# An encoder layer: six products of the values ahead of a branch, four of them read behind it; the sums of X on VectorE; two small PSUM banks for three uses

## The chip, the core and the metric

The kernel runs on one core of one Trainium2 chip. The metric is the device time of one execution in microseconds. A core has five engines with their own instruction queues: TensorE (PE in the profile, with PEld for its weight loads), VectorE (DVE), ScalarE (ACT), GpSimd (POOL) and SyncE (SP), which here issues the transfers. They meet through semaphores. TensorE writes into PSUM, which has eight banks of 128 x 512 float32; VectorE and ScalarE read them.

## The reference

One layer of a bidirectional encoder over x of 2048 x 1024 float32, then a final RMSNorm:

```python
h = _rmsnorm(x, norm_w[layer])
proj = jnp.einsum('bsd,de->bse', h, w_in[layer])           # 1024 -> 10 x 1024 columns
(q_raw, ffwd_raw, fbwd_raw, i_raw, ga_raw,
 u_raw, v_raw, gb_raw, ma_raw, mb_raw) = jnp.split(proj, split_points, axis=-1)
y_a = _hgrn2_branch(q_raw, ffwd_raw, fbwd_raw, i_raw, ga_raw, ...)   # gated linear recurrence, both ways
# branch B:
u = jax.nn.gelu(u_raw)
v = _layernorm(jax.nn.gelu(v_raw), ln_w, ln_b)
mixed = jnp.einsum('gts,bnsgc->bntgc', w_s, vc) + b_s.T[None, None, :, :, None]
y_b = u * mixed.reshape(b, s, SG_WIDTH) * jax.nn.silu(g_raw)
merged = (jax.nn.sigmoid(ma_raw) * jnp.einsum('bsw,wd->bsd', y_a, w_proj_a[layer])
          + jax.nn.sigmoid(mb_raw) * jnp.einsum('bsw,wd->bsd', y_b, w_proj_b[layer]))
x = x + jnp.einsum('bsd,de->bse', merged, w_out[layer])
return _rmsnorm(x, final_norm_w)
```

## The kernel before

The normed x lies transposed in SBUF as four tiles xT of 512 positions, each value as the sum of two float16 numbers (high and low part). A product of two such operands takes three matmuls for each 128 rows of the contraction (high x high, high x low, low x high).

The stages follow one another on TensorE:

1. `phase1` (lines 297 to 423): the columns of the recurrence, and the recurrence itself. At its end the first two products of the values are made (`self.first`).
2. `values` (827 to 894): the columns `v_raw`, 16 tiles of 128 positions in two halves of 512 columns. A half is one product of 24 matmuls into a bank of the pool `p_v` (five banks, tile `pin`), read by ScalarE with the gelu into a tile V (three buffers); VectorE takes the statistics (line 844); after the second half VectorE aggregates them, GpSimd makes the reciprocal deviation (850, 851), VectorE norms the tile (852) and SP stores it to DRAM (854).
3. `branch_b`: gates and mixing. `merge_gates`: the two merge gates. `branch_a`: the gate path of the recurrence. `final`: the projections, the merge, the output.

**The branch.** The recurrence is computed by a short way that holds while its numbers stay in a range. Behind the products of three tiles (`early = 3`, lines 856 to 862) `range_flag` loads a flag into a register on every engine, and `exact()` repeats the recurrence in a safe way where the flag is set. With these inputs it isn't set. Each engine has a branch instruction there, and then an instruction that sets its semaphore as if the block had run. In `exact` too, products go through the five banks of `pin`.

**Seven products.** From `branch_b` on, a product of 2 x 2 blocks is made with seven block products (Winograd's form), written out in `seven` (752): twelve matmuls each into one of three banks of a side, which `copy` and `take` read on ScalarE and VectorE. That needs sums of blocks of both operands. For X these are made beside the values: `x_parts(p, k)` (613) adds the high and low parts of X into a buffer `raw` (two adds on GpSimd, line 619), makes the sums there (`z_sums`, three operations on VectorE, line 642) and splits them into high and low parts (ScalarE 626, VectorE 627). `raw` and `tmp` have one buffer each. `x_last(p, k)` (629) makes the last sum in place in xT. For weights and for later operands the class `Make` (658) does the like: `load` (DMA), `square` and `scale` (a common power of two, from the sum of squares), `sums`, `split`. Its steps are hung into slots: `side_by_side` (797) runs product n of each generator and then the functions in slot n.

**Small PSUM tiles.** `scale` (718) adds up over the partitions with a matmul into the bank `misc` (one buffer), which VectorE reads (`pow2`, line 130). `px` (one buffer) takes the mixing products of branch B (957, read by 959), the bias (900) and the transposes of branch A (1162, read by 1164). With the six banks of the seven products that makes eight.

**The order.** Tile, the library the kernel is written in, plans each engine's order ahead of time: it runs the program through a cost model, gives each engine what is ready, first what comes first in the program, and writes a fixed order with all semaphore waits. An instruction may so be planned ahead of one that stands before it in the program. At run time every engine works through its list in that order.

Of the kernel before, what the change touches and what calls it, by code (L numbers as in the profile page):

```python
# [17 lines left out]
F32 = mybir.dt.float32  # L18
# [6 lines left out]
PSUM = bass.MemoryType.PSUM  # L25
# [26 lines left out]
class Trunk:  # L52
# [9 lines left out]
    def consts(self):  # L62
        nc, tc, ctx = self.nc, self.tc, self.ctx
        c = self.c = ctx.enter_context(tc.tile_pool(name="consts", bufs=1))
        self.sm = ctx.enter_context(tc.tile_pool(name="small", bufs=4))
        self.dram = ctx.enter_context(tc.tile_pool(name="scratch", bufs=1, space=DRAM))
        self.pg = ctx.enter_context(tc.tile_pool(name="p_misc", bufs=1, space=PSUM))
        self.plan()

        self.ident = c.tile([P, P], F32, name="ident")  # L70
        make_identity(nc, self.ident)
        self.ones = c.tile([P, P], F32, name="ones")
        nc.vector.memset(self.ones, 1.0)
        self.ones16 = c.tile([P, P], BF16, name="ones16")
        nc.vector.memset(self.ones16, 1.0)
        self.mhalf = c.tile([P, 1], F32, name="mhalf")
        nc.vector.memset(self.mhalf, -0.5)
# [535 lines left out]
    def x_parts(self, p, k):  # L613

        nc = self.nc
        raw, tmp = self.rt.tile([P, 2, 2, SEG], F32, name="raw"), self.rt.tile([P, 3, SEG], F32, name="tmp")
        for i in range(2):
            x = self.xT[2 * p + i]
            nc.gpsimd.tensor_tensor(out=raw[:, :, i], in0=x[:, 0, 2 * k:2 * k + 2], in1=x[:, 1, 2 * k:2 * k + 2],
                                    op=ALU.add)  # L620
        flat = raw.rearrange("p h i t -> p (h i) t")
        self.z_sums(flat, tmp, s3=False)
        xs = self.xs[p][k // 2]
        for dst, src in ((slice(0, 1), flat[:, 1:2]), (slice(1, 3), tmp[:, 1:3])):
            hi, lo = (xs[:, a, dst, k % 2] for a in range(2))
            nc.scalar.activation(out=hi, in_=src, func=AF.Copy)
            nc.vector.tensor_tensor(out=lo, in0=src, in1=hi, op=ALU.subtract)

    def x_last(self, p, k):

        nc = self.nc
        r = self.vw.tile([P, 2, SEG], F32, name="V")
        xs = [self.xT[2 * p + i][:, :, 2 * k] for i in range(2)]
        for i in range(2):
            nc.vector.tensor_tensor(out=r[:, i], in0=xs[i][:, 0], in1=xs[i][:, 1], op=ALU.add)
        nc.vector.tensor_tensor(out=r[:, 0], in0=r[:, 0], in1=r[:, 1], op=ALU.subtract)
        nc.scalar.activation(out=xs[1][:, 0], in_=r[:, 0], func=AF.Copy)
        nc.vector.tensor_tensor(out=xs[1][:, 1], in0=r[:, 0], in1=xs[1][:, 0], op=ALU.subtract)

    def z_sums(self, raw, tmp, s3=True, part=(0, 1)):  # L640

# [16 lines left out]
    class Make:  # L658
# [3 lines left out]
            self.s, self.inv = scale or (None, None)  # L662

        def load(self):
            self.raw = self.rt.tile([P, 2, 1024], F32, name="raw")
            self.tmp = self.rt.tile([P, 3, SEG], F32, name="tmp")
            self.flat = self.raw.rearrange("p h n -> p (h n)")
            self.src(self.raw)

        def square(self):  # L670
            sm, tr = self.tr.sm, self.tr
            ss = sm.tile([P, 2], F32, name="wss2")
            junk = self.tmp.rearrange("p i n -> p (i n)").bitcast(F16)
            for h in range(2):
                self.nc.scalar.activation(out=junk[:, 1024 * h:1024 * h + 1024], in_=self.raw[:, h],  # L675
                                          func=AF.Square, accum_out=ss[:, h:h + 1])
            self.sb = sm.tile([P, 2], BF16, name="wsb2")
            self.nc.gpsimd.tensor_copy(out=self.sb, in_=ss)
# [2 lines left out]
            self.s, self.inv = self.tr.scale([self.sb[:, i:i + 1] for i in range(2)], ("ws7", "winv7"), 12)  # L681

        def sums(self, i):
            if self.kind == "z":
                return self.tr.z_sums(self.raw.rearrange("p h (i t) -> p (h i) t", i=2), self.tmp, part=(i,))
            b11, b12, b21, b22 = self.blocks
            t2, t3, t4 = (self.tmp[:, j] if len(b11.shape) == 2 else
                          self.tmp[:, j].rearrange("p (k n) -> p k n", n=P) for j in range(3))
            sub = lambda out, x, y: self.nc.vector.tensor_tensor(out=out, in0=x, in1=y, op=ALU.subtract)  # L689
            if i == 0:  # L690
                sub(t3, b22, b12)
                sub(b12, b12, b11)
            else:
                sub(t2, b22, b12)
                sub(t4, b21, t2)
# [22 lines left out]
    def scale(self, sums, names, bufs):  # L718

        nc, sm = self.nc, self.sm  # L720
        pb = self.pg.tile([P, 1], F32, name="misc")
        for i, sb in enumerate(sums):
            nc.tensor.matmul(pb, self.ones16, sb, start=(i == 0), stop=(i == len(sums) - 1))  # L723
        s = sm.tile([P, 1], F32, name=names[0], bufs=min(bufs, 3))
        inv = sm.tile([P, 1], F32, name=names[1], bufs=bufs)
        self.pow2(s, inv, pb, room=1)
        return s, inv

    def make_w(self, w, c0, u, rt, scale=None):

# [96 lines left out]
    def values(self):  # L827
# [1 line left out]
        wv = [self.wv, self.unit(self.w_in, C_V + SEG, ahead=0)]  # L829
        V, st, order = {}, {}, self.v_order  # L830

        def half(t, u):
            b, n = order[t] // 4, order[t] % 4
# [3 lines left out]
            if u == 0 and t < len(self.first):  # L837
                ps = self.first[t]
            else:
                ps = self.pin.tile([P, SEG], F32, name="pin")  # L840
                self.proj_wide(ps, wv[u][0], self.xT[b], slice(n * P, n * P + P))
            v = V[t][:, 4 * u:4 * u + 4].rearrange("p g c -> p (g c)")
            nc.scalar.activation(out=v, in_=ps, func=AF.Gelu_apprx_tanh, scale=wv[u][1])  # L843
            nc.vector.bn_stats(out=st[t][:, u], in_=v)
            if u == 0:
# [5 lines left out]
            nc.gpsimd.tensor_tensor(out=r, in0=r, in1=self.mhalf, op=ALU.pow)  # L851
            nc.vector.tensor_scalar(out=V[t], in0=V[t], scalar1=mv[:, 0:1], scalar2=r,
                                    op0=ALU.subtract, op1=ALU.mult)
            nc.sync.dma_start(out=self.v_d[b][:, :, n, :], in_=V[t])

        early = 3
        for u in range(2):
            for t in range(early):
                half(t, u)
        flag = self.range_flag()  # L860
        with tc.If(flag > 0):
            self.exact()
        right = dict(side="right", reuse_waits="tile")
        xs = self.ctx.enter_context(tc.tile_pool(name="xs", bufs=4, **right))
        self.xsp = xs
# [3 lines left out]
        self.own = [self.make_w(*x) for x in self.x_units()]  # L869
        first, second = self.own[0:2]  # L870
        for t in range(early, NT):
            for u in range(2):
                half(t, u)

            if 3 <= t < 11:
                self.x_parts((t - 3) // 4, (t - 3) % 4)
            if 7 <= t < 15:
                self.x_last((t - 7) // 4, (t - 7) % 4)
            if t == 11:
                first.load()  # L880
            elif t == 12:
                first.square()
                first.scale()
            elif t == 13:
                first.sums(0)
                first.sums(1)
            elif t == 14:
                for i in range(4):
                    first.split(i, self.w7)
# [6 lines left out]
    def mixing_bias(self, i, wsT, bsb):  # L896

        nc = self.nc
        pr = self.pq.tile([P, 4, P], F32, name="px")
# [28 lines left out]
    def branch_b(self):  # L928

        nc, tc, sm = self.nc, self.tc, self.sm  # L930
        with ExitStack() as es:
# [16 lines left out]
            for u in range(4):  # L948
                y = {}
                order = [(p, i, j) for i, j in ((0, 0), (1, 1), (0, 1), (1, 0)) for p in range(2)]  # L950
                def mix(p, i, j):
                    b, g = 2 * p + i, 2 * u + j
                    v = vl.tile([P, 4, P], F32, name="vl")
                    nc.sync.dma_start(out=v, in_=self.v_d[b][:, g])
                    px = self.pq.tile([P, 4, P], F32, name="px")
                    for n in range(4):
                        nc.tensor.matmul(px[:, n, :], v[:, n, :], wsT[:, g, :], start=True, stop=True)
                    y[p, i, j] = yp.tile([P, 4, P], F32, name="y")
# [67 lines left out]

    def make_z(self, kind, p, k, rt):
        src = lambda raw: self.nc.sync.dma_start(out=raw, in_=self.y_d[kind][p][k].rearrange("p h i t -> p h (i t)"))
        return self.Make(self, src, rt, self.zscale[kind, p], "z")

    def merge_gates(self):

# [123 lines left out]
    def ga_group(self, side, p, u, unit):  # L1156
        nc = self.nc

        def turn(o, sg, i, j):
            pt = self.pq.tile([P, 4, P], F32, name="px")  # L1160
            for n in range(4):
                nc.tensor.transpose(pt[:, n, :], o[:, n, :], self.ident)
            y = o.rearrange("p n t -> p (n t)")
# [32 lines left out]
    def final(self, z, last):  # L1196
# [4 lines left out]
        for n in range(6):  # L1201
# [4 lines left out]
            else:  # L1206
                zk = ((1, 0), (1, 1), (2, 0), (2, 1), None)[n - 1]
                zn = [None] * 4
                if zk:
                    self.z_scale(*zk)  # L1210
                    mk = [self.make_z(*zk, k, self.rt) for k in range(4)]
                    mk[0].load()
            xo = None
            for u in range(4):
                slots = {}
# [3 lines left out]
                if mk:  # L1219
                    m = mk[u]  # L1220

                    def begin(m=m):
# [2 lines left out]
                        pool = next(self.z_from)  # L1225
                        m.split(0, pool)

                    slots = {1: [begin], 2: [lambda m=m: m.split(1)], 3: [lambda m=m: m.split(2)],
                             4: [lambda m=m: m.split(3)] + ([mk[u + 1].load] if u < 3 else [])}
                if kind < 2:  # L1230
                    if W[u] is None:
                        W[u] = self.pb[3].t, self.pb[3].inv
# [193 lines left out]
    def run(self):  # L1426
# [14 lines left out]
        self.mb_d = blocks("mb")  # L1441
        self.kept, self.zscale, self.rot = {}, {}, [(0, 1, 2), (0, 1, 2)]
        self.xTp = ctx.enter_context(tc.tile_pool(name="xTp", bufs=NSEG))
        with tc.tile_pool(name="p_in", bufs=2, space=PSUM) as self.pin, tc.tile_pool(name="wu", bufs=5) as self.wu:
            self.phase1()
            with tc.tile_pool(name="p_v", bufs=5, space=PSUM, reuse_waits="tile") as self.pin, \
                    tc.tile_pool(name="vw", bufs=3, reuse_waits="tile") as self.vw:
# [52 lines left out]
```

## Time and profile before

| | |
|---|---|
| time, median of 3 runs | 2433.22 us (2428.64 to 2433.70) |
| the profiled execution: its own time | 2434.28 us |
| its span, first to last instruction | 2432.5 us |
| TensorE busy | 2334.8 us |
| VectorE / ScalarE / GpSimd busy | 1535.1 / 1020.4 / 315.9 us |
| mean granted TensorE clock | 0.992 |
| moved by DMA | 281.26 MB |

Times in the profile count from the first instruction. A row of a timeline has the start, the duration, the engine, the line of the kernel, the operation, the tile it writes and those it reads, the shapes, the count, and in brackets the idle time of that engine ahead of it with what ended it. A row by line has the count, shortest, median and longest duration in ns, and first and last start. A row of a list of waits has who waited for whom, the total, the count and the longest. The suffix q on an engine means its sequencer. A row of a stretch has start and end, its length, and then for each engine the busy time and count.

### The profile page before, as it was taken

Reading aid. Unit: us, or ns where it says so; the run is one execution under the profiler, and the core shown is the slowest. Engines: PE = TensorE matmul, PEld = TensorE weight load, DVE = VectorE, ACT = ScalarE, POOL = GpSimd, SP = SyncE. Lnnn points to the kernel's source line nnn. Section 1 sums busy time; section 2 is a strip of 40 time slices with the busy share of each in tenths; the row PEclk is TensorE's granted clock in tenths of the full one; section 3 lists DMA queues with packets and bytes.
Section 4 is the critical chain, followed back from the end, with each engine's and each line's share of the span. In section 5 each row is a group of like instructions: output and inputs, shape, how many; then the busy total and the mean of one; then the engine's idle time right before and its main releaser. Section 6 shows DMA issues by size and latency. Waiting matters only on the chain. (4 is left out here: it accounts for less than half of the span.)

```text
span 2432.5 us, 33850 instructions
## 1 busy us (share of the span) xinstructions
PE 2334.8 (96%) x12880; PEld 1299.2 (53%) x12880; DVE 1535.1 (63%) x3014; ACT 1020.4 (42%) x1871; POOL 315.9 (13%) x523
## 2 busy tenths in 40 slices
PE   7999999999999999899999999899999999999998
PEld 5666766685668566444444554344444444444443
DVE  5687548745872677567456456577765554576754
ACT  6533332433332334323345446566564532244432
POOL 2222202220211121351000000000000000000011
PEclk9999999999999999999999999999999999999999
DMA  5200110011001001112322222677665674777733
GB/s 176 77 10 27 36 35 10 27 36 36 14 23 47 6 18 53 46 52 79 121 88 90 83 87 95 221 260 265 245 201 171 215 268 148 276 239 263 241 122 119
DMA packets 169486, 281.26 MB, mean 116 GB/s; under 512 B 10976, under 2 KB 105184, under 8 KB 162144
## 3 DMA queue, kind: packets, MB, share of 16 engines
q1 hardware_dynamic: 169312, 278.98, 33.7%
q8 instruction: 104, 1.70, 0.3%
q14 instruction: 70, 0.57, 0.1%
HBM read 174.08 MB, written 104.86 MB: 115 GB/s over the span
## 5 line engine op out<-in xcount | busy, mean ns | idle before, releaser
L794 PEld LDWEIGHTS <-seven 128*128 128x128 f16 x5376 | 525.4, 98 | 640.5 <-issue 32.0
L794 PE MATMUL bank<-seven 128*128 128x512 f16 x2016 | 441.2, 381 | 8.7 <-DVE zs L808 6.4
L794 PE MATMUL bank<-xT,seven 128*128 128x512 f16 x1920 | 429.3, 380 | 4.8 <-ACT zs L761 2.6
L794 PE MATMUL bank<-xs,seven 128*128 128x512 f16 x1440 | 321.1, 380 | 0.0
L217 PE MATMUL pin<-xT,wsplit 128*128 128x512 f16 x768 | 291.1, 379 | 0.2 <-DVE wsplit L204 0.2
L215 PE MATMUL pin<-xT,wsplit 128*128 128x512 f16 x768 | 291.0, 379 | 0.2 <-ACT xT L279 0.2
L216 PE MATMUL pin<-xT,wsplit 128*128 128x512 f16 x768 | 291.1, 379 | 0.0
L215 PE MATMUL pin<-wsplit,xT 128*128 128x256 f16 (+1 forms) x768 | 240.3, 313 | 9.5 <-ACT V L843 5.0
L216 PE MATMUL pin<-wsplit,xT 128*128 128x256 f16 (+1 forms) x768 | 240.7, 313 | 3.2 <-DVE wsplit L204 3.2
L217 PE MATMUL pin<-wsplit,xT 128*128 128x256 f16 (+1 forms) x768 | 240.5, 313 | 2.3 <-DVE xT L280 2.1
L808 DVE SCALAR_TENSOR_TENSOR zs<-bank,us,zs 128x512 f32<-128x512 f32 x120 | 88.9, 746 | 76.6 <-PE bank L794 74.0
L815 ACT ACTIVATE zs<-zs 128x512 f32<-128x512 f32 x120 | 75.3, 627 | 140.0 <-DVE zs L808 139.7
L808 DVE SCALAR_TENSOR_TENSOR zs<-bank,su,zs 128x512 f32<-128x512 f32 x72 | 53.9, 749 | 110.0 <-PE bank L794 86.4
L217 PEld LDWEIGHTS <-wsplit 128*128 128x128 f16 x768 | 75.1, 98 | 90.2 <-DVE wsplit L204 0.7
L502 POOL TENSOR_TENSOR q<-ff,e 128x512 f32<-128x512 f32 x64 | 73.6, 1150 | 371.7 <-DVE e L500 231.0
L216 PEld LDWEIGHTS <-wsplit 128*128 128x128 f16 x768 | 75.1, 98 | 77.5
L215 PEld LDWEIGHTS <-wsplit 128*128 128x128 f16 x768 | 75.4, 98 | 75.7
L689 DVE TENSOR_TENSOR tmp<-raw 128x512 f32<-128x512 f32 x64 | 43.9, 690 | 111.9 <-ACT tmp L675 104.5
L455 ACT ACTIVATE fz<-pin,wus 128x512 f32<-128x512 f32 x64 | 43.9, 686 | 143.1 <-PE pin L217 142.9
L761 ACT ACTIVATE zs<-bank,us 128x512 f32<-128x512 f32 x120 | 80.1, 676 | 56.0 <-PE bank L794 53.5
L216 PEld LDWEIGHTS <-xT 128*128 128x128 f16 x768 | 76.5, 100 | 44.7 <-issue 9.7
L217 PEld LDWEIGHTS <-xT 128*128 128x128 f16 x768 | 76.4, 99 | 44.2 <-DVE xT L280 5.0
(202 smaller groups left out, 3614.5 us busy)
## 6 DMA issues: line engine op xcount, KB each, us to landing
kept<-seven SPq DMA_DIRECT2D x16, 1792.0 KB, 7.9
seven<-kept SPq DMA_DIRECT2D x16, 1792.0 KB, 9.4
wraw<-in_w_in_dram SPq DMA_DIRECT2D x20, 1024.0 KB, 5.1
raw<-in_w_in_dram SPq DMA_DIRECT2D x40, 512.0 KB, 4.8
xt<-in_x_dram SPq DMA_DIRECT2D x16, 512.0 KB, 4.2
o_d<-ob SPq DMA_DIRECT2D x32, 256.0 KB, 2.3
v<-V SPq DMA_DIRECT2D x16, 512.0 KB, 3.5
vl<-v SPq DMA_DIRECT2D x32, 256.0 KB, 2.8
```

Of the source, the lines that this page charges most:

```text
L215: nc.tensor.matmul(ps, lh(k), rh(k), start=(k == 0), stop=False)
L216: nc.tensor.matmul(ps, lh(k), rl(k), start=False, stop=False)
L217: nc.tensor.matmul(ps, ll(k), rh(k), start=False, stop=(k == KT - 1))
L455: nc.scalar.activation(out=fz[:, 1:SEG + 1], in_=ps, func=AF.Sigmoid, scale=us)
L502: nc.gpsimd.tensor_tensor(out=q0.rearrange("p (m c) -> p m c", c=64), in0=ff.rearrange("p (m c) -> p m c", c=64), in1=e8.rearrange("p n b ...
L689: sub = lambda out, x, y: self.nc.vector.tensor_tensor(out=out, in0=x, in1=y, op=ALU.subtract)
L761: self.nc.scalar.activation(out=t, in_=ps, func=AF.Copy, scale=su)
L794: nc.tensor.matmul(ps, lhs(x, k), rhs(y, k), start=start and not (k or n), stop=k == 3 and n == 2, skip_group_check=True)
L808: self.nc.vector.scalar_tensor_tensor(out=more, in0=ps, scalar=su, in1=more, op0=ALU.mult, op1=ALU.add)
L815: self.nc.scalar.activation(out=out, in_=more, func=func)
```

## The change

Four things are changed.

- `values`: `half` is split into `product` (the matmuls) and `norm` (gelu, statistics, norming, store). Six products are still made ahead of the branch, but only the two that `phase1` made are read there; the other four are read behind `exact()`.
- `x_parts` and `x_last` become generators of two steps, one after each half of a tile; the two adds of `x_parts` go from GpSimd to VectorE. `x_last` runs one tile later (tiles 8 to 15), and so does the scale of the first weight unit.
- The bank `misc` lives until the end of the values. From then on `scale` takes its bank from the pool of `px`, which gets two buffers.
- `Make.load` takes only `raw`; `tmp` is taken when it is first needed. In `final`, a piece is begun at slot 2 in place of 1 (but for the fourth unit), the next is loaded one slot earlier, after the second split, and the first piece of the next group is loaded in slot 4 of the fourth unit, ahead of its scale.

```diff
     def x_parts(self, p, k):
...
-            nc.gpsimd.tensor_tensor(out=raw[:, :, i], in0=x[:, 0, 2 * k:2 * k + 2], in1=x[:, 1, 2 * k:2 * k + 2],
+            nc.vector.tensor_tensor(out=raw[:, :, i], in0=x[:, 0, 2 * k:2 * k + 2], in1=x[:, 1, 2 * k:2 * k + 2],
                                     op=ALU.add)
         self.z_sums(flat, tmp, s3=False)
+        yield
...
         def load(self):
-            self.raw = self.rt.tile([P, 2, 1024], F32, name="raw")
-            self.tmp = self.rt.tile([P, 3, SEG], F32, name="tmp")
+            self.raw, self.tmp = self.rt.tile([P, 2, 1024], F32, name="raw"), None
...
     def scale(self, sums, names, bufs):
-        pb = self.pg.tile([P, 1], F32, name="misc")
+        pb = self.px()[:, 0, 0:1] if self.pq else self.pg.tile([P, 1], F32, name="misc")
...
+    def px(self):
+        return self.pq.tile([P, 4, P], F32, name="px", bufs=2)
...
         early = 3
+        ps = {}
         for u in range(2):
             for t in range(early):
-                half(t, u)
+                ps[t, u] = product(t, u)
+                if u == 0 and t < len(self.first):
+                    norm(t, u, ps[t, u])
         flag = self.range_flag()
         with tc.If(flag > 0):
             self.exact()
+        for t in range(early):
+            for u in range(int(t < len(self.first)), 2):
+                norm(t, u, ps[t, u])
...
         for t in range(early, NT):
+            parts = ([self.x_parts((t - 3) // 4, (t - 3) % 4)] if 3 <= t < 11 else []) + \
+                    ([self.x_last((t - 8) // 4, (t - 8) % 4)] if 8 <= t else [])
             for u in range(2):
-                half(t, u)
-            if 3 <= t < 11:
-                self.x_parts((t - 3) // 4, (t - 3) % 4)
-            if 7 <= t < 15:
-                self.x_last((t - 7) // 4, (t - 7) % 4)
+                norm(t, u, product(t, u))
+                for x in parts:
+                    next(x)
             if t == 11:
                 first.load()
             elif t == 12:
                 first.square()
+            elif t == 13:
                 first.scale()
-            elif t == 13:
                 first.sums(0)
...
     def final(self, z, last):
-                    mk[0].load()
+                    early.s, early.inv = mk[0].s, mk[0].inv
+                    mk[0] = early
...
-                    slots = {1: [begin], 2: [lambda m=m: m.split(1)], 3: [lambda m=m: m.split(2)],
-                             4: [lambda m=m: m.split(3)] + ([mk[u + 1].load] if u < 3 else [])}
+                    at = 2 if u < 3 else 1
+                    slots = {at: [begin], at + 1: [lambda m=m: m.split(1)], at + 2: [lambda m=m: m.split(2)],
+                             at + 3: [lambda m=m: m.split(3)]}
+                    if u < 3:
+                        slots[at + 1].append(mk[u + 1].load)
+                if u == 3 and n < 4:
+                    early = self.make_z(*((1, 0), (1, 1), (2, 0), (2, 1))[n], 0, self.rt)
+                    slots.setdefault(4, []).append(early.load)
...
-        with tc.tile_pool(name="p_in", bufs=2, space=PSUM) as self.pin, tc.tile_pool(name="wu", bufs=5) as self.wu:
+        self.pq = None
+        with tc.tile_pool(name="p_misc", bufs=1, space=PSUM, reuse_waits="tile") as self.pg, \
+                tc.tile_pool(name="p_in", bufs=2, space=PSUM) as self.pin, tc.tile_pool(name="wu", bufs=5) as self.wu:
```

More of the change, by code (lines that the diff above doesn't have):

```diff
@@ L627, in x_parts @@
             nc.vector.tensor_tensor(out=lo, in0=src, in1=hi, op=ALU.subtract)
+        yield
     def x_last(self, p, k):
@@ L636, in x_last @@
         nc.vector.tensor_tensor(out=r[:, 0], in0=r[:, 0], in1=r[:, 1], op=ALU.subtract)
+        yield
         nc.scalar.activation(out=xs[1][:, 0], in_=r[:, 0], func=AF.Copy)
         nc.vector.tensor_tensor(out=xs[1][:, 1], in0=r[:, 0], in1=xs[1][:, 0], op=ALU.subtract)
+        yield
     def z_sums(self, raw, tmp, s3=True, part=(0, 1)):
@@ L664, in load, with need @@
         def load(self):
-            self.raw = self.rt.tile([P, 2, 1024], F32, name="raw")
-            self.tmp = self.rt.tile([P, 3, SEG], F32, name="tmp")
+            self.raw, self.tmp = self.rt.tile([P, 2, 1024], F32, name="raw"), None
             self.flat = self.raw.rearrange("p h n -> p (h n)")
             self.src(self.raw)
+        def need(self):
+            if self.tmp is None:
+                self.tmp = self.rt.tile([P, 3, SEG], F32, name="tmp")
         def square(self):
+            self.need()
             sm, tr = self.tr.sm, self.tr
@@ L683, in sums @@
         def sums(self, i):
+            self.need()
             if self.kind == "z":
@@ L830, in values, with product, norm @@
         V, st, order = {}, {}, self.v_order
-        def half(t, u):
-            b, n = order[t] // 4, order[t] % 4
+        def product(t, u):
+            if u == 0 and t < len(self.first):
+                return self.first[t]
+            ps = self.pin.tile([P, SEG], F32, name="pin")
+            self.proj_wide(ps, wv[u][0], self.xT[order[t] // 4], slice(order[t] % 4 * P, order[t] % 4 * P + P))
+            return ps
+        def norm(t, u, ps):
             if u == 0:
@@ L836, in half @@
                 st[t] = sm.tile([P, 2, 6], F32, name="bst")
[L837 to L841, printed above, removed]
             v = V[t][:, 4 * u:4 * u + 4].rearrange("p g c -> p (g c)")
@@ L853, in half @@
                                     op0=ALU.subtract, op1=ALU.mult)
-            nc.sync.dma_start(out=self.v_d[b][:, :, n, :], in_=V[t])
+            nc.sync.dma_start(out=self.v_d[order[t] // 4][:, :, order[t] % 4, :], in_=V[t])
         early = 3
+        ps = {}
         for u in range(2):
             for t in range(early):
-                half(t, u)
+                ps[t, u] = product(t, u)
+                if u == 0 and t < len(self.first):
+                    norm(t, u, ps[t, u])
         flag = self.range_flag()
@@ L898, in mixing_bias @@
         nc = self.nc
-        pr = self.pq.tile([P, 4, P], F32, name="px")
+        pr = self.px()
         nc.tensor.matmul(pr, self.ones, wsT[:, 4 * i:4 * i + 4, :], start=True, stop=True)
@@ L954, in mix @@
                     nc.sync.dma_start(out=v, in_=self.v_d[b][:, g])
-                    px = self.pq.tile([P, 4, P], F32, name="px")
+                    px = self.px()
                     for n in range(4):
@@ L1028, in make_z @@
         src = lambda raw: self.nc.sync.dma_start(out=raw, in_=self.y_d[kind][p][k].rearrange("p h i t -> p h (i t)"))
-        return self.Make(self, src, rt, self.zscale[kind, p], "z")
+        return self.Make(self, src, rt, self.zscale.get((kind, p)), "z")
     def merge_gates(self):
@@ L1159, in turn @@
         def turn(o, sg, i, j):
-            pt = self.pq.tile([P, 4, P], F32, name="px")
+            pt = self.px()
             for n in range(4):
```

1 line of the change is left out of this document (removed).

## The prediction

> **What bounds the kernel now.** I read the page first, then TensorE's list of waits, then the stretches around the edits.
>
> ```profile
> span 2432.5 us, 33850 instructions
> PE 2334.8 (96%) x12880; PEld 1299.2 (53%) x12880; DVE 1535.1 (63%) x3014; ACT 1020.4 (42%) x1871; POOL 315.9 (13%) x523
> ```
>
> TensorE (PE) is busy for all but 97.7 us (2432.5 - 2334.8), and no matmul is removed. So a gain can only come out of those 97.7 us, or out of matmuls that ran at a lowered clock just behind a pause. The list of TensorE's waits says which part of them the edits touch:
>
> ```profile
> PE bank L794 <- DVE zs L808: 8.5, 8, 2.1
> PE px L957 <- DVE y L959: 7.8, 4, 3.7
> PE pin L215 <- ACT V L843: 5.0, 3, 3.1
> PE bank L794 <- ACT zs L761: 4.9, 8, 0.9
> PE misc L723 <- DVE p2t L130: 4.5, 1, 4.5
> PE pin L215 <- ACTq L861: 4.5, 1, 4.5
> PE px L1162 <- DVE zs L1164: 4.0, 5, 1.6
> ```
>
> The columns are the wait in total, how often, and the longest. Rows 2 and 7 are the one px bank, row 5 the one misc bank, row 6 the branch, row 3 the sums of X. Rows 1 and 4 are spread over the stages of the seven products, most of them in the last one.
>
> **The branch.** The sequencers' rows of line 861, two of TensorE's timeline, one of ScalarE's:
>
> ```profile
> L861 PEldq COMPARE_BRANCH  x1: 4883/4883/4883, 1010.0 to 1010.0; - x1
> L861 POOLq COMPARE_BRANCH  x1: 45/45/45, 1011.7 to 1011.7; - x1
> L861 POOLq EVENT_SEMAPHORE  x1: 17/17/17, 1014.7 to 1014.7; - x1
> L861 ACTq COMPARE_BRANCH  x1: 50/50/50, 1014.8 to 1014.8; - x1
> L861 PEldq EVENT_SEMAPHORE  x1: 51/51/51, 1015.0 to 1015.0; - x1
> L861 ACTq EVENT_SEMAPHORE  x1: 17/17/17, 1017.9 to 1017.9; - x1
> 1013.50 0.69 ACT L843 ACTIVATE V<-pin,wus 128x512 f32<-128x512 f32 x1 [4.28 <-PE pin L217]
> 1017.95 0.38 PE L215 MATMUL pin<-wsplit,xT 128*128 128x512 f16 x1 [4.49 <-ACTq L861]
> 1021.79 0.38 PE L216 MATMUL pin<-wsplit,xT 128*128 128x512 f16 x1
> ```
>
> TensorE is through its own branch at 1015.0 but starts at 1017.95, when ScalarE has passed: ScalarE had to read the sixth product (1013.50) before it could branch (1014.8), and an engine needs about 3 us from branch to next instruction (GpSimd 1011.7 to 1014.7, ScalarE 1014.8 to 1017.9). The edit moves four reads (ScalarE), their four statistics and three tile norms (VectorE, GpSimd) and three stores of V (SP's queue) behind the branch. All engines but TensorE can then branch while the products run, so that TensorE waits for its own branch alone: 1015.0 in place of 1017.95, 2.9 us.
>
> The pause also costs clock. From 1017.95 to 1021.79 ten matmuls took 3.84 us. At full speed they are 0.2157 us apart, from the row of 24:
>
> ```profile
> 1161.45 5.34 PE L794 MATMUL bank<-xT,seven 128*128 128x512 f16 x24
> ```
>
> (5.34 - 0.38) / 23 = 0.2157, so ten are 2.16 us and 1.7 us were lost. A pause of 1.6 us (1013.46 to 1015.0) should not lower it: after the pause of 1.67 quoted below the matmul is at 0.38. Together 4.6 us; bounds 0 (if the reads stay in front) and 4.6.
>
> The Trainium skill (Advanced Engine Details and Errata, Control Flow Timing) gives about 108 ns for a compare-and-branch. By it ScalarE would have been through at 1014.9, and this term would be 0 and the time 4.6 us higher. The rows disagree: 3.1 us on ScalarE, 3.0 on GpSimd. The skill's page Runtime: NRT & Kernel Launch (Instruction fetch mechanics) has a taken branch out of the loaded pages wait for a fetch, which fits them.
>
> **The sums of X.** GpSimd's adds move to VectorE, in steps:
>
> ```profile
> L619 POOL TENSOR_TENSOR raw<-xT x16: 2116/2129/3111, 1018.0 to 1081.0; 128x1024 f32<-128x1024 f16 x16
> 1079.32 2.76 DVE L627 TENSOR_TENSOR xs<-tmp,xs 128x1024 f16<-128x1024 f32 x1 [0.52 <-ACT xs L626]
> 1087.90 1.23 DVE L627 TENSOR_TENSOR xs<-tmp,xs 128x1024 f16<-128x1024 f32 x1 [1.12 <-ACT xs L626]
> L642 DVE TENSOR_TENSOR tmp<-raw x56: 679/691/694, 1024.3 to 2318.4; 128x512 f32<-128x512 f32 x56
> L844 DVE BATCH_NORM_STATS2 bst<-V x32: 671/686/697, 992.5 to 1162.3; 128x6 f32<-128x512 f32 x32
> L852 DVE TENSOR_SCALAR V<-V,bmv,lrs x16: 811/812/814, 1008.1 to 1164.2; 128x1024 f32<-128x1024 f32 x16
> 1079.91 0.59 PE L215 MATMUL pin<-wsplit,xT 128*128 128x512 f16 x1 [3.13 <-ACT V L843]
> 1083.20 0.38 PE L217 MATMUL pin<-wsplit,xT 128*128 128x512 f16 x1
> 1088.49 0.38 PE L215 MATMUL pin<-wsplit,xT 128*128 128x512 f16 x1 [1.67 <-ACT V L843]
> ```
>
> Eight parts follow one another through one buffer. Each has two GpSimd adds, and VectorE's last operation takes 2.76 us beside the next adds against 1.23 when none run. ScalarE's copies wait for VectorE with the products' reads behind them in its queue, so that the five banks fill: TensorE stands 3.13 + 1.67 us, and 8 matmuls from 1079.91 to 1083.20 take 3.29 in place of 1.73 us. That is 6.4 us.
>
> An add on VectorE is not in the trace; the nearest row of that size, line 627 undisturbed, has 1.23 us. A part is then 2 x 1.23 + 3 x 0.69 + 0.69 + 1.23 = 6.4 us of VectorE, eight 52. The stretch holds 16 products, 16 x 24 x 0.2157 = 83 us. VectorE's share besides: eight tiles at 2 x 0.69 + 0.81 = 2.2, 17.5 in all; the held norms, 4 x 0.69 + 3 x 0.81 = 5.2; and three last sums of four operations each, 8.3. Together 83, as much as TensorE has, with four banks (20.7 us) as a reserve. That fits without being comfortable, since an engine that waits in order also loses time between parts. Bounds: 6.4 gained; or lost 16 x 1.23 less 8 x 1.5 that the last operations give back = 7.7. I take half of the gain, 3.2. The last sums one tile later, and the scale of the first unit one tile later, lie under tiles 13 to 15, where no pause of TensorE is listed: 0. If that cover is gone, branch B's first group waits for its unit.
>
> The Trainium skill (Perfetto Trace Analysis, Optimizing Scalar/DVE Operations) warns that GpSimd and VectorE share a read port, so that shifting work between them might not help. By that this term is 0 and the time 3.2 us higher. The 2.76 against 1.23 shows the contention it speaks of; whether the shift helps no row here shows.
>
> **The two small banks.** Mixing products, turns and scale products now share two. The first mixing stall:
>
> ```profile
> 1175.89 0.69 DVE L689 TENSOR_TENSOR tmp<-raw 128x512 f32<-128x512 f32 x1 [5.58 <-ACT tmp L675]
> 1172.67 1.05 PE L957 MATMUL px<-wsT,vl 128*128 128x128 f32 x8
> 1178.75 2.08 PE L957 MATMUL px<-wsT,vl 128*128 128x128 f32 x8 [3.73 <-DVE y L959]
> 1180.62 4.79 PE L794 MATMUL bank<-xs,seven 128*128 128x512 f16 x18
> ```
>
> VectorE stands behind the weights' sums, and the second of a pair of mixes waits for the read of the first. With two banks the pair goes through: 7.8 us of waits. The clock adds 2.08 - 1.05 = 1.0, and on the 18 matmuls 4.79 - (17 x 0.2157 + 0.38) = 0.7. Sum 9.6; bounds 0 and 9.6; I take it all, since the next pair comes two groups later.
>
> ```profile
> 1550.10 0.65 POOL L678 CAST wsb<-wss 128x2 bf16<-128x2 f32 x1 [22.25 <-ACT tmp L675]
> 1554.00 0.20 PE L723 MATMUL misc<-wsb,ones 128*128 128x1 bf16 x2 [4.50 <-DVE p2t L130]
> 1554.07 11.56 PE L794 MATMUL bank<-xT,seven 128*128 128x512 f16 x45
> ```
>
> Here two scale products collide in the misc bank. With a second bank the product waits only for its cast: the pause runs from 1549.50 to 1550.75, 3.2 us less. The 45 matmuls behind it took 11.56 against 44 x 0.2157 + 0.38 = 9.9, so 1.7 more. Sum 4.9. The turns wait 4.0 in all; scale products now alternate with turns in the same two banks, so I take half, 2.0 (bounds: 4.0 gained, 4.0 lost, as scales may wait as long as turns did). A scale could also hold the bank that branch B's first group wants; the longest wait for a scale's read is the 4.5 above, the planner can put the other side's group first, and I take 0.
>
> **The last stage.** The pieces of z are begun one slot later, the next is loaded after the second split, and the next stage's first piece is loaded in the slots of the fourth unit.
>
> ```profile
> 1975.00:2432.50 457.50, 435.94 (x1998) 195.76 (x1996) 271.77 (x381) 155.80 (x266) 31.02 (x72) 0.99 0.61 208
> 2085.17 0.32 SPq L1028 DMA_DIRECT2D raw<-ya  x1
> L1265 DVE TENSOR_TENSOR zs<-zs x32: 681/684/693, 2131.5 to 2275.7; 128x512 f32<-128x512 f32 x32
> L716 DVE SCALAR_TENSOR_TENSOR seven<-raw,zs,seven x48: 1274/1280/1287, 1593.8 to 2322.7; 128x1024 f16<-128x1024 f32 x48
> L716 DVE SCALAR_TENSOR_TENSOR seven<-tmp,zs,seven x48: 1007/1012/1020, 1599.6 to 2324.8; 128x768 f16<-128x768 f32 x48
> ```
>
> TensorE is idle for 21.6 us of the first row's stretch (457.50 - 435.94). The first piece made in the group of units whose first result comes at 2131.5 was already issued at 2085.17, 46 us ahead: the planner pulls a load forward as soon as its buffer is free, past SP's other transfers and whatever its slot. So the new slots are worth 0; bounds 13.4 gained (rows 1 and 4 of the waits) and the loss of the slower rival below.
>
> **Sum.** 4.6 + 3.2 + 9.6 + 4.9 + 2.0 = 24.3 us. The profiled execution's own time is 2434.3 (1.8 above its span), and 1.1 above the median shown, 2433.2. 2434.3 - 24.3 = 2410.0; I forecast **2410 us**, own range 2403 to 2417.
>
> **Rivals.**
> - *VectorE paces the values* (chance 0.20). For: 83 us of work in 83 us, and in-order copies ahead of the reads. Against: five banks of slack, and no lock against GpSimd. Nothing of the 3.2 is gained and up to 7.7 lost: 2413 to 2421, say 2417. The warning quoted above from the Trainium skill (Perfetto Trace Analysis) ends at the lower of the two.
> - *The last stage gains too* (0.15). For: its waits are on VectorE's and ScalarE's reads, which stand behind pieces. Against: the pull forward. About 10 of the 13.4: 2400.
> - *The branch stays as long* (0.10): the change doesn't do what it says there, because TensorE's 4.883 us begin anew behind its last matmul, or the planner leaves reads in front. 2410 + 4.6 = 2415. The 108 ns of the Trainium skill (Advanced Engine Details and Errata) end here too.
> - *Slower: VectorE in the last stage* (0.08). Begun at slot 2, a piece has four sums and a split there, 4 x 0.69 + 1.28 = 4.04 us against a slot of 12 x 0.2157 = 2.59, and splits in slots 3, 4 and 5, each with a result to take: three operations of about 0.7 where there are two gates. 2.1 + 1.28, 2.1 + 1.01 and 2.1 + 1.01 against 2.59 leave VectorE 1.45 + 0.8 + 0.5 + 0.5 = 3.2 us late. It decides from one slot of delay on (2.59), where a bank is wanted back: 12 pieces, of which six have the shorter takes (1.45 + 0.1 = 1.6 late), make up to 6 x 3.2 + 6 x 1.6 = 29 us: 2439. For: there are waits for banks there now. Against: slots do not place the pieces, as the load at 2085 shows.
> - The rest, 0.47, is the forecast.
>
> **Range and chances.** 2398 to 2429 takes in the gain of the last stage, the VectorE case and the branch case, and leaves out the slower one and surprises. A difference of 0.2% (4.9 us) is about what can be told from none: faster 0.88 (all cases but the slower, with a little off), within 0.2% 0.05, slower 0.07.
>
> **What would show it.** The branch: TensorE's first matmul behind it within 2 us of the sixth product, at 0.38 us. The sums: line 619 on VectorE near 1.23 us, line 627 never above 1.3, no wait of pin for V. The banks: no wait of px for y, the wait of line 723 for p2t gone, those of turns down to about 2 us. The last stage: idle still about 21 us. I am wrong if the pauses come back under other names, above all as waits for VectorE between 1015 and 1090 or behind 1975.

## The result, and the profile after

The changed kernel takes 2413.9 us (median of four runs, 2408.2 to 2417.9) against 2431.7 of the kernel before on the same chip: ratio 0.992, 95% interval 0.991 to 0.993. A second job gave 2409.4 (2405.2 to 2413.7; ratio 0.991, 0.989 to 0.993). 2410 was forecast, with a range of 2403 to 2417. The gain is 17.8 us in the first job and 20.2 in the second, where the kernel before took 2429.6.

The first rows of the changed kernel's page, and its list of TensorE's waits (total, how often, longest):

```profile
span 2406.5 us, 33836 instructions
...
PE 2327.8 (97%) x12880; PEld 1296.7 (54%) x12880; DVE 1538.3 (64%) x3030; ACT 1022.1 (42%) x1871; POOL 276.2 (11%) x507
```

```profile
PE bank L805 <- DVE zs L819: 8.2, 10, 2.0
...
PE px L731 <- POOL wsb L685: 6.2, 2, 3.6
PE pin L214 <- ACTq L877: 4.2, 1, 4.2
...
PE bank L805 <- ACT zs L772: 3.0, 6, 0.7
...
PE px L1181 <- DMA zs<-o_d: 2.5, 3, 1.1
...
PE px L731 <- POOL zsb L1043: 2.1, 2, 1.9
...
PE px L976 <- DMA vl<-v: 1.5, 1, 1.5
```

Lines have moved: the branch is 877 (861 before), the gelu 855 (843), the adds of X 618 (619), the scale product 731 (723), the seven products 805 (794), the mixing products 976 (957), the turns 1181 (1162). Gone are the waits of `pin` for V, of `px` for y and of the scale product for `p2t`. Still there is the wait at the branch, 4.2 in place of 4.5.

Cut at the starts of matmuls in the timelines, the stages in us (pause: start of the sixth product's last matmul to start of the first behind the branch; values: from there to branch B's first seven-product matmul):

| kernel | pause | values | branch B | merge gates | branch A | last stage |
|---|---|---|---|---|---|---|
| before | 4.87 | 143.5 | 332.4 | 303.7 | 170.6 | 464.4 |
| changed | 4.55 | 136.7 | 322.8 | 300.9 | 168.7 | 460.3 |
| changed, second profile | 4.42 | 137.1 | 322.9 | 300.7 | 169.2 | 465.0 |

Up to branch A these two profiles of the changed kernel agree within 0.5 us. The gains are 0.3 at the branch, 6.8 in the values, 9.7 in branch B, 2.9 in the merge gates, 1.9 in branch A: 21.6. The last stage repeats less well, and so does branch A in the runs below, in kernels that don't touch it. Rows of its stretch, of the kernel before, of the changed kernel and of its second profile:

```profile
1968.20:2432.50 464.30, 442.01 (x2029) 198.90 (x2027) 278.11 (x390) 161.79 (x275) 31.02 (x72) 0.99 0.61 209
```

```profile
1946.20:2406.50 460.30, 440.36 (x2029) 198.38 (x2027) 277.97 (x392) 162.32 (x275) 29.64 (x72) 0.99 0.61 211
```

```profile
1946.90:2411.90 465.00, 442.16 (x2029) 198.84 (x2027) 277.64 (x392) 162.00 (x275) 31.33 (x72) 0.99 0.60 209
```

TensorE is idle in it for 22.3, 19.9 and 22.8 us (length less the first busy time).

### The profile page after: what moved, and what is told of

It reads as the page before. It is cut to its first block, busy times and chain, and to the rows that moved or that the text cites. A ratio compares the mean times of both kernels' runs of the same rounds, so it can differ in the third digit from the quotient of the medians.

```text
span 2406.5 us, 33836 instructions
## 1 busy us (share of the span) xinstructions
PE 2327.8 (97%) x12880; PEld 1296.7 (54%) x12880; DVE 1538.3 (64%) x3030; ACT 1022.1 (42%) x1871; POOL 276.2 (11%) x507
## 5 line engine op out<-in xcount | busy, mean ns | idle before, releaser
L216 PEld LDWEIGHTS <-xT 128*128 128x128 f16 x768 | 76.1, 99 | 44.1 <-DVE xT L279 4.9
L458 DVE TENSOR_SCALAR fz<-fz,fb,fa 128x512 f32<-128x512 f32 x64 | 35.6, 557 | 97.9 <-ACT fz L454 97.9
```

The lines of the kernel that those rows point to most:

```text
L216: nc.tensor.matmul(ps, ll(k), rh(k), start=False, stop=(k == KT - 1))
L458: nc.vector.tensor_scalar(out=f, in0=f, scalar1=fb, scalar2=fa, op0=ALU.mult, op1=ALU.add)
```

## The experiments

### The same kernel again, and the last stage's slots

> The changed kernel as it is, a second time, as the yardstick for the stages. If the gain of each stage belongs to the change, the stretches between the marks repeat within 1 us: from the first product behind the branch to branch B 136.7, branch B 322.8, the merge gates 300.9, branch A 168.7, the last stage 460.3. If the 4 us that the last stage gained are only the spread from one execution to the next, that stretch comes out nearer to the 464.4 of before. Time 2414, within 5.

Measured: 2409.4 (2405.2 to 2413.7). Of one and the same program the last stage took 465.0 here and 460.3 in the first profile, with 464.4 in the kernel before between them. So the 4 us are within the spread of executions.

In the next kernel the last stage's slots are as before:

```diff
-                    early.s, early.inv = mk[0].s, mk[0].inv
-                    mk[0] = early
+                    mk[0].load()
...
-                    at = 2 if u < 3 else 1
+                    at = 1
...
-                        slots[at + 1].append(mk[u + 1].load)
-                if u == 3 and n < 4:
-                    early = self.make_z(*((1, 0), (1, 1), (2, 0), (2, 1))[n], 0, self.rt)
-                    slots.setdefault(4, []).append(early.load)
+                        slots[at + 3].append(mk[u + 1].load)
```

> The changed kernel with the old slots of the last stage: a piece begun at slot 1, the next loaded after the fourth split, no load ahead of the group. My prediction's theory: a load is pulled forward whatever its slot, so the last stage stays at 460 and the time at 2414; what it gained is then the spread between executions, or comes from how the earlier stages end. Rival: slots and early load made the gain: the last stage goes to 464 and the time to 2418.

Measured: 2410.8 (2409.4 to 2412.8; ratio 0.992, 0.991 to 0.994), last stage 462.0, between the two profiles of the changed kernel. Over all kernels here, the last stage took 459.3 to 465.0 in the ten profiles with the new slots and 462.0 to 464.4 in the three with the old ones. No effect of the slots shows; one of 2 or 3 us couldn't.

### The adds of X

The adds alone back on GpSimd in the changed kernel (`nc.vector.tensor_tensor` to `nc.gpsimd.tensor_tensor` in `x_parts`), and the adds alone on VectorE in the kernel before, without the two steps.

> The changed kernel with the two adds of a part of X back on GpSimd, the two steps kept. My theory: GpSimd's adds (2.1 us each) delay the part and stretch VectorE's last operation from 1.23 to 2.76 us, so the waits of the products for the reads (3.1 + 1.7 us) and the slow matmuls behind them come back: 136.7 goes to 143, the time up by 6.4 to 2420. Rival: the two steps, which let the second half's read in between, made the gain: the stretch stays at 137 and the time at 2414.

> The kernel before with one part alone: the two adds of a part of X on VectorE, without the two steps. My theory: it gives the whole gain of the values: 143.5 goes to 137, the time from 2430 to 2423. Rival: without the steps the adds and sums of a part stand in one block ahead of the second half's statistics, the reads' buffers fill, and the stretch stays at 140 or above.

Measured: on GpSimd 2418.7 (ratio 0.996, 0.994 to 0.997), values 144.0; alone on VectorE in the kernel before 2421.3 (ratio 0.996, 0.994 to 0.997), values 136.5. The rows of the add and of VectorE's last operation, first of the changed kernel, then with the adds on GpSimd:

```profile
L618 DVE TENSOR_TENSOR raw<-xT x16: 1172/1218/1226, 1017.1 to 1076.2; 128x1024 f32<-128x1024 f16 x16
L627 DVE TENSOR_TENSOR xs<-tmp,xs x8: 1217/1218/1222, 1027.8 to 1082.1; 128x1024 f16<-128x1024 f32 x8
```

```profile
L618 POOL TENSOR_TENSOR raw<-xT x16: 2116/2126/3111, 1019.9 to 1082.9; 128x1024 f32<-128x1024 f16 x16
L627 DVE TENSOR_TENSOR xs<-tmp,xs x8: 1225/2228/2765, 1029.3 to 1089.8; 128x1024 f16<-128x1024 f32 x8
PE pin L214 <- ACT V L855: 5.0, 3, 3.2
```

The move of the adds is the whole gain of this part: it takes the 5.0 us of waits and the median of line 627 from 2.2 to 1.2 us. The two steps add nothing that shows.

### The two small banks

```diff
-        pb = self.px()[:, 0, 0:1] if self.pq else self.pg.tile([P, 1], F32, name="misc")
+        pb = self.pg.tile([P, 1], F32, name="misc")
...
-        return self.pq.tile([P, 4, P], F32, name="px", bufs=2)
+        return self.pq.tile([P, 4, P], F32, name="px", bufs=1)
```

with `p_misc` open to the end of the kernel.

> The changed kernel with one bank for mixing products and turns and one for the scales, as before. My theory: the second mixing product waits for the read of the first again. Branch B goes from 322.8 to 332.4, the merge gates from 300.9 to 303.8, branch A from 168.7 to 170.6, the time from 2414 to 2428. Rival: part of the 9.7 us of branch B came from the sums of X, which leave VectorE less behind at its start; then branch B comes out at 327 or less and the time at 2420.

Measured: 2426.0 (ten runs; ratio 0.998, 0.997 to 0.999); branch B 332.1, merge gates 303.4, branch A 171.3, the other stages as in the changed kernel. The waits are back under their old names:

```profile
PE px L976 <- DVE y L978: 7.4, 4, 3.3
...
PE px L1181 <- DVE zs L1183: 4.3, 5, 1.6
PE misc L731 <- DVE p2t L129: 4.0, 1, 4.0
```

Against the mean of the two profiles of the changed kernel, branch B loses 9.2 and the merge gates 2.6 us. That 11.8 is this part's gain as far as it is shown: over all kernels here that leave these stages alone otherwise, branch B took 321.9 to 322.9 with the two banks for three uses and 332.1 to 332.5 without, the merge gates 299.6 to 301.0 and 303.4 to 303.7.

Branch A comes out 2.4 us longer, but this isn't shown to be the banks. It took 167.8 to 172.1 us in ten profiles with the new banks and 168.8, 170.6 and 171.3 in three with the old ones.

### The branch

First the reads written ahead of the branch again, and nothing else:

```diff
-                if u == 0 and t < len(self.first):
-                    norm(t, u, ps[t, u])
+                norm(t, u, ps[t, u])
         flag = self.range_flag()
         with tc.If(flag > 0):
             self.exact()
-        for t in range(early):
-            for u in range(int(t < len(self.first)), 2):
-                norm(t, u, ps[t, u])
```

> The changed kernel with the reads of all six products written ahead of the branch again, as before. My theory after the result: this part of the change moves nothing, because the safe way repeated in the branch takes its banks from the same five as the held products, so the reads have to stand ahead of it on ScalarE wherever they are written. Then TensorE's pause at the branch stays at 4.3 to 4.8 us and the time at 2412, within 4. Rival (the prediction): the split moves the reads behind; then the pause, 4.5 in the changed kernel, grows by 2 or more here.

Measured: 2410.5 (2409.2 to 2414.7; ratio 0.991, 0.990 to 0.993), pause 4.9. With the safe way's banks as they are, where the reads are written moves nothing that shows. In the changed kernel all four run ahead of the branch, as its timeline of ScalarE (the last read), the sequencers' rows and the first matmuls behind show:

```profile
1012.97 0.69 ACT L855 ACTIVATE V<-pin,wus 128x512 f32<-128x512 f32 x1 [4.28 <-PE pin L216]
```

```profile
L877 PEldq COMPARE_BRANCH  x1: 4861/4861/4861, 1009.5 to 1009.5; - x1
...
L877 ACTq COMPARE_BRANCH  x1: 50/50/50, 1014.3 to 1014.3; - x1
L877 PEldq EVENT_SEMAPHORE  x1: 51/51/51, 1014.4 to 1014.4; - x1
...
L877 ACTq EVENT_SEMAPHORE  x1: 17/17/17, 1017.0 to 1017.0; - x1
```

```profile
1017.10 0.58 PE L214 MATMUL pin<-wsplit,xT 128*128 128x512 f16 x1 [4.16 <-ACTq L877]
1017.48 0.63 PE L215 MATMUL pin<-wsplit,xT 128*128 128x512 f16 x1
...
1020.35 0.38 PE L216 MATMUL pin<-wsplit,xT 128*128 128x512 f16 x1
```

`exact()` takes its tiles `pin` and `po` from the five banks that hold the unread products. In the next kernel it takes them from the two banks of phase 1's products, which are read ahead of the branch in any case; and the four reads are tied to the block by their scale, which ScalarE copies ahead of the branch and again inside the block:

```diff
             self.phase1()
+            self.pin0 = self.pin
...
-            pin = self.pin
+            pin = self.pin0
...
-                            po = self.pin.tile([1, 4, P], F32, name="po", tag="pin")
+                            po = self.pin0.tile([1, 4, P], F32, name="po", tag="pin")
...
         flag = self.range_flag()
+        hs = sm.tile([P, 2], F32, name="hs", bufs=1)
+        hold = lambda: [nc.scalar.activation(out=hs[:, u:u + 1], in_=wv[u][1], func=AF.Copy) for u in range(2)]
+        hold()
         with tc.If(flag > 0):
             self.exact()
+            hold()
...
-                norm(t, u, ps[t, u])
+                norm(t, u, ps[t, u], hs[:, u:u + 1])
```

> The changed kernel, with the safe way behind the branch given the two banks of the first two products (read ahead of it), and the scale of the four held reads copied again by ScalarE inside the branch's block and copied ahead of it, so that the reads cannot be planned in front. My theory: ScalarE is through its branch before TensorE is, TensorE waits for its own branch alone, and resumes some 1.9 to 2.2 us after its last matmul instead of 4.5, with matmuls at 0.38 us: 2.5 us plus 1.0 to 1.7 of clock, 2409 in place of 2412. Rival 1: TensorE's own branch begins anew or another engine takes ScalarE's place, the pause stays at 4.3 or more and the time at 2412. Rival 2: four reads in a row behind a table load of 1.3 us make VectorE late, and a wait of the values' products comes back behind 1025.

Measured: 2401.8 (2399.5 to 2402.9; ratio 0.987, 0.986 to 0.989), 8.7 less than the kernel with the reads written ahead, run in the same job. The sequencers' rows and the matmuls around the branch:

```profile
L880 ACTq COMPARE_BRANCH  x1: 50/50/50, 998.7 to 998.7; - x1
...
L880 ACTq EVENT_SEMAPHORE  x1: 17/17/17, 1001.4 to 1001.4; - x1
...
L880 PEldq COMPARE_BRANCH  x1: 3352/3352/3352, 1009.5 to 1009.5; - x1
L880 PEldq EVENT_SEMAPHORE  x1: 51/51/51, 1013.0 to 1013.0; - x1
```

```profile
1012.53 0.38 PE L216 MATMUL pin<-wsplit,xT 128*128 128x512 f16 x1
1013.06 0.38 PE L215 MATMUL pin<-wsplit,xT 128*128 128x512 f16 x1
```

ScalarE is through at 1001.4 and TensorE hardly pauses: 0.53 us between two starts, of which it is idle for 0.15. TensorE's own branch, issued at 1009.5, is over by 1013.0, when the matmuls queued ahead of it have run. From the sixth product's last matmul to branch B it is 135.0 us, against 141.3 in the changed kernel.

The edit does one thing more. The product behind the branch starts with line 214, but the first matmul behind the branch is one of line 215. The values' matmuls that start ahead of the branch are 1684 here and 1680 in the changed kernel, and all 2304 of the kernel's matmuls of this form are on record in both. So TensorE makes the first four of that product ahead of the branch, in a stretch where it otherwise waits for the weights of the second half:

```profile
995.63 0.39 PE L214 MATMUL pin<-wsplit,xT 128*128 128x512 f16 x1
995.86 0.38 PE L215 MATMUL pin<-wsplit,xT 128*128 128x512 f16 x1
996.08 0.38 PE L216 MATMUL pin<-wsplit,xT 128*128 128x512 f16 x1
996.29 0.38 PE L214 MATMUL pin<-wsplit,xT 128*128 128x512 f16 x1
997.57 0.38 PE L215 MATMUL pin<-wsplit,xT 128*128 128x512 f16 x1 [0.90 <-DVE wsplit L203]
```

In the changed kernel that wait is 1.88 us.

Is it the banks or the tie? The banks alone, with the reads written behind the branch and then ahead of it (one run each):

> The changed kernel with the safe way given the first two products' banks, but without the copied scale that holds the reads. It tells apart what keeps the reads in front. If the banks alone do, all four reads stand behind the branch, the pause is gone (first matmul within 0.6 us) and the time is near 2402. If the planner, which gives ScalarE what is ready, does it as well, ScalarE still reads up to three of the four ahead of its branch at about 1009, and TensorE's pause shrinks without going: 0.5 to 2.5 us.

> The fourth case beside three that have run: the safe way has its own banks, but the reads of all six products are written ahead of the branch. If both are needed, the order of the program and the banks, ScalarE reads all four ahead of its branch and TensorE's pause is 4.3 to 4.9 us, the time 2412 within 5. If the banks alone were what mattered, the pause is 1.8 or less and the time 2403.

Measured: 2403.6 and 2403.3, pause 1.82 and 1.84. My expectation for the second, that both are needed, fell: at the branch the banks alone matter, and what is written where does not. ScalarE's timeline and the sequencers' rows of the first, and TensorE's resumption in the first and in the second:

```profile
1006.50 0.69 ACT L855 ACTIVATE V<-pin,wus 128x512 f32<-128x512 f32 x1 [2.55 <-PE pin L216]
1009.55 1.28 ACT L855 ACT_TABLE_LOAD   x1 [2.37 <-ACTq L877]
1011.46 0.69 ACT L855 ACTIVATE V<-pin,wus 128x512 f32<-128x512 f32 x1 [0.62 <-PE pin L216]
```

```profile
L877 ACTq COMPARE_BRANCH  x1: 50/50/50, 1007.0 to 1007.0; - x1
L877 PEldq COMPARE_BRANCH  x1: 4712/4712/4712, 1008.0 to 1008.0; - x1
```

```profile
1012.86 0.38 PE L215 MATMUL pin<-wsplit,xT 128*128 128x512 f16 x1 [1.44 <-PEq L877]
```

```profile
1014.92 0.38 PE L215 MATMUL pin<-wsplit,xT 128*128 128x512 f16 x1 [1.46 <-PEq L876]
```

Three of the four reads still precede the branch. One read behind it is enough: ScalarE branches at 1007.0, before the sixth product is done, and TensorE waits for its own branch alone. In both kernels, too, the first four matmuls of the next product run ahead of the branch (from 994.14 in the first), before any engine has branched. So the bank that they fill no longer hangs on the block or on ScalarE's way through it. Not told apart: how much of the shorter pause comes from that, and how much from ScalarE's earlier branch.

### The scale of the merge gates

```diff
                 if m.inv is None:
                     m.square()
-                    m.scale()
                 m.sums(0)
...
             def end(e, i):
                 m = made[e]
+                if m.inv is None:
+                    m.scale()
```

In TensorE's written order the scale products of the four units of `w_proj_a` stand 24 matmuls later.

> The changed kernel with the scale product of the merge gates' units made with the splits, one slot later, instead of right behind the squares. My theory: the 2.58 and 3.64 us that this product still waits for its cast come from weights that land late, with the products of the gates queued behind it on TensorE; 24 matmuls later (5.2 us) the cast is there. The merge gates go from 300.8 to 294, the time from 2412 to 2405. Rival: the split behind the scale becomes late, holds the unit's buffer and with it the next load, and the wait moves to the next unit: 300 or more.

Measured: 2403.2 (2401.3 to 2404.5; ratio 0.988, 0.987 to 0.990), 7.3 less than with the reads written ahead in the same job; merge gates 295.2 in place of 300.8, branch A 167.8. Rows of the changed kernel's timeline, then what is left in this kernel's list of waits:

```profile
1508.73 1.06 ACT L682 ACTIVATE tmp<-raw 128x1024 f16<-128x1024 f32 x1 [2.07 <-DMA raw<-in_w_proj_a_dram]
...
1510.70 0.19 PE L731 MATMUL px<-wsb,ones 128*128 128x1 bf16 x2 [2.58 <-POOL wsb L685]
...
1550.66 1.06 ACT L682 ACTIVATE tmp<-raw 128x1024 f16<-128x1024 f32 x1 [1.78 <-DMA raw<-in_w_proj_a_dram]
...
1552.63 0.19 PE L731 MATMUL px<-wsb,ones 128*128 128x1 bf16 x2 [3.64 <-POOL wsb L685]
```

```profile
PE px L731 <- POOL wsb L685: 1.1, 1, 1.1
```

The cast was late because the square of the second half waited for the weights (2.07 and 1.78 us); TensorE stood at the scale product with the gates' products behind it.

### Both together

The edits of the held reads with own banks and of the later scale, in one kernel:

> The changed kernel with both of the edits that helped: the safe way's own banks with the four reads held behind the branch, and the merge gates' scale products with the splits. My theory: the two gains lie in different stages and add up, 8 to 9 us and 7 to 8 us against the changed kernel's 2410 to 2414, to about 2396: no pause at the branch, 135 from the sixth product to branch B, merge gates at 295. Rival: the last stage or another wait takes part of it back, and the time stays at 2401, that of the better of the two.

Measured: 2396.1 (four runs, 2391.3 to 2402.9; ratio to the kernel before 0.986, 0.983 to 0.988). The gains add, as far as the spread lets it be told: 0.39 us of idle time at the branch, 135.1 from the sixth product to branch B, merge gates 295.7. Its last stage was 463.7 in the profiled execution, 2402.9, the longest of the four.

## Why the prediction was right, and where its steps were wrong

The total was right, 2413.9 and 2409.4 against 2410, both inside the range. Part of this is luck. Of the terms, the branch and the merge gates came out 4.3 and 2.0 short and the sums of X 3.6 over, so that the misses nearly cancelled. And I counted a gain of 24.3 us down from 2434.3, while the gains measured, 17.8 and 20.2, start from 2431.7 and 2429.6. The 2415 of the rival in which the branch stays as long fits the first median better than 2410 does.

**The branch (4.6 forecast, 0.3 found): wrong.** The step that failed is "the edit moves four reads behind the branch". It moves them in the text only. What happened is the rival with a chance of 0.10, in its second form: reads stay in front. I gave it as a habit of the planner. The planner does put up to three reads in front, but the runs show that the banks of `exact()` decide: with banks of its own the pause falls to 1.8 whichever way the reads are written. The rest of the step held: with ScalarE through early, TensorE waits 1.44 us for its own branch, and the matmuls behind it take 0.38 us, as worked out (1.6 and no loss of clock). It even erred low: with the other engines through by 1005 the pause all but vanishes, and 6.3 us are gained, 141.3 less 135.0. Of these 4.0 are the pause (4.55 less 0.53) and 1.5 the clock (eight matmuls from 1017.10 to 1020.35 took 3.25 us in place of 8 x 0.2157 = 1.73). The four matmuls made ahead of the branch are worth 4 x 0.2157 = 0.9, which is the rest to within 0.1; the prediction had no such term.

The compare-and-branch of about 108 ns that the Trainium skill gives (Advanced Engine Details and Errata, Control Flow Timing) would have ended this term at 0 too, but for another reason than the trace's: ScalarE still takes 2.7 us from its branch to its next instruction (1014.3 to 1017.0, and 998.7 to 1001.4).

**The sums of X (3.2 forecast, 6.8 found): right in mechanism, half in size.** The add takes 1.22 us on VectorE, where the nearest row had 1.23, and line 627 never more than 1.22. My doubt was VectorE's room. It was busy for 33.26 of 38 us where the parts are densest, which left enough. The row of that stretch, and that of the last sums' adds:

```profile
1022.00:1060.00 38.00, 38.00 (x178) 17.21 (x176) 33.26 (x45) 14.97 (x19) 3.23 (x6) 1.00 0.14 43
```

```profile
L636 DVE TENSOR_TENSOR V<-xT x16: 679/684/689, 1083.3 to 1150.4; 128x512 f32<-128x512 f16 x16
```

TensorE is busy throughout the stretch, at a granted clock of 1.00. The estimate of 83 us against 83 charged three last sums to the stretch of the parts; they come from 1083.3 on, when the last part's operation (line 627, 1082.1) has begun. Halving the gain for that was the error. The shared read port that the Trainium skill warns of (Perfetto Trace Analysis, Optimizing Scalar/DVE Operations) would account for the 2.2 us of line 627 beside GpSimd's adds. That a shift might not help did not come true here: with the adds on VectorE line 627 takes 1.22.

**The two banks (9.6, 4.9 and 2.0 forecast; 9.7, 2.9 and 1.9 found): right in branch B, too large in the merge gates, not shown in branch A.** Putting the old banks back costs 9.2 and 2.6 in the first two. The 1.9 of branch A agrees with the forecast but shows nothing, since that stage varies by 4.3 us between kernels that have the same banks. In branch B the new wait for a V from DRAM is only 1.5. In the merge gates the mis-sized part is the residual wait: I let the cast be ready 1.25 us after TensorE comes (1549.50 to 1550.75); it came 3.64 late, because TensorE got there with the weights still on their way. The collision of two scale products is gone, as predicted, but the load is what is late next.

**The last stage (0 forecast): right,** as far as it can be told. The 4 us of the first profile went away in the second, and undoing the slots gave 462.0. The slower rival, VectorE late by three splits in a row, didn't come; neither did the gain of 10.

## What to carry to other kernels

Reads that shall come behind a branch, and products that shall run ahead of it, need banks that the branch's block doesn't also use; a resource shared with code that never runs still orders what does. When a collision in a bank is taken away, ask when its operand arrives, and place the product that needs it behind that arrival, so that TensorE's queue isn't held by it. Profile the same program more than once before a gain of 0.2% in a long stage is put down to an edit, and look at that stage in all the kernels that leave it alone.

## What the runs showed of the hardware that was not expected

TensorE's branch took 4.86 us in the changed kernel, where GpSimd, VectorE and SyncE branched between 1011.2 and 1012.1, 4.71 where they did so between 1009.6 and 1010.6, and 3.35 and 3.63 where they had branched before 1005. It looks as if branches taken at the same time slow one another; no run varied that alone. The branch runs beside the matmuls already queued: the one of 3.35 us left TensorE idle for 0.15 us, that of 3.63 for 0.39.

Pauses of 1.44, 1.46 and 1.67 us left the matmuls behind them at 0.38 us. At 1.87 it went either way. The wait for the second half's weights ahead of the branch lasts 1.86 to 1.88 us in nine profiles. Slow matmuls follow it in three of them (the changed kernel, the adds on GpSimd, the old slots), where the first ten take 1.0 to 1.7 us more than at full speed, and none in the other six. First the kernel before, then the changed one:

```profile
998.33 0.38 PE L216 MATMUL pin<-wsplit,xT 128*128 128x512 f16 x1 [1.87 <-DVE wsplit L204]
998.54 0.38 PE L217 MATMUL pin<-wsplit,xT 128*128 128x512 f16 x1
```

```profile
996.19 0.48 PE L215 MATMUL pin<-wsplit,xT 128*128 128x512 f16 x1 [1.88 <-DVE wsplit L203]
996.47 0.63 PE L216 MATMUL pin<-wsplit,xT 128*128 128x512 f16 x1
```

The first matmul behind a pause doesn't tell it: behind the pause of 4.49 us of the kernel before it still took 0.38, and the next two 0.53 and 0.63.

One program's last stage took 460.3 and 465.0 us in two executions, a spread of 0.2% of the whole time.
